# Sorting the partial products of a split-precision matmul: all high x high ones first

## The chip, the cores and the metric

The kernel runs on one core of a Trainium2 chip. The metric is the time of one execution on the device, in microseconds; the median of three runs stands for a kernel. Each kernel has one profiled execution besides, from which the trace and the profile page come. PE is TensorE (matmuls), DVE is VectorE, ACT is ScalarE, POOL is GpSimd, SP is the engine that issues most of the DMAs.

## The reference

A decoder trunk of two layers over 512 tokens of width 1024, in fp32. Layer 0 mixes tokens by attention with a forget gate, layer 1 by a gated short convolution. Each layer then has an MLP of width 4096 with squared ReLU and a gate stage that adds a per-layer embedding. Cut to what matters here:

```python
def sq_relu_mlp(h, w_up, w_down):
    return jnp.square(jax.nn.relu(h @ w_up)) @ w_down

for i in range(DEPTH):                                  # DEPTH = 2
    ...                                                 # mixer, residual
    f = sq_relu_mlp(rmsnorm(x, g[2]), w_mlp_up[i], w_mlp_down[i])
    x = x + rmsnorm(f, g[3])
    gate = jax.nn.sigmoid(rmsnorm(x, g[4]) @ w_ple_gate[i])
    e = (p[i] @ w_ple_proj[i]) * gate
    x = x + rmsnorm(e, g[5])
```

## The kernel before

**Split products.** Every fp32 operand is split into a high part, which ACT makes with a cast (line 272), and a low part, the difference, which DVE or POOL makes with a subtraction (line 273); a `Pair` holds both. A product is three matmuls into one PSUM bank, which `mm3` issues for one term after another: high x high (line 264), low x high (line 265), high x low (line 266). Names in the trace end in h and l for the two parts: wh and wl are a weight's, hTh and hTl those of the normed, transposed hidden state, A12h and A12l those of a quarter of the activations.

**The MLP** goes in 8 groups of 512 of the 4096 hidden columns. `up` makes four blocks f = 0 to 3 of 128 hidden columns each; block f takes 8 terms (k = 0 to 7) into a bank `up`. Group 0 does this in two chunks of 256 tokens, all four blocks of the first chunk and then all of the second; the other groups take all 512 tokens at once. ACT empties the bank with a ReLU into a page r (line 820) and squares r into a page q (line 806).

For groups 0 to 6 the down-projection is a scheme of seven products in place of eight (Strassen-Winograd). Its left factors are quarters of the activations and their sums: A11, A12, A22 and S1 to S4; blocks 0 and 1 give the first tile of each, blocks 2 and 3 the second (the last) tile. `quarters` has POOL make the sums s (line 834), and `halves` splits them. Its right factors are quarters of the weights and their sums T1 to T4, which POOL makes in `derive` (line 167) and of which POOL also makes the low parts. `down` runs the steps in the order `STEPS` = (1, 2, 4, 5, 6, 7, 3); each step is one product: two halves of tokens s, each with a bank `dn`, and two tiles p, four terms or 12 matmuls of 512 columns in all. Step 1 takes A11, steps 2 and 4 the quarters A12 and A22, which are split together under the name A12, step 5 takes S1, step 6 S2, split with S1, and steps 7 and 3 take S3 and S4. In group 0 ACT copies the finished banks into pages acc (line 863), in groups 1 to 6 DVE adds them to acc (line 866). Group 7 is plain and `combine` puts the products together.

**The gate stage** `ple` runs 8 blocks in the order `BLOCKS`, 8 terms each into a bank `pg`.

**What sets the order.** There are 8 PSUM banks, given out in turn, so a new step needs a bank that an earlier result has left. The MLP and gate stages aren't ordered by hand: a scheduler takes the program as written, with an estimate of its times, and moves each engine's instructions; each engine then works its list off in order, waiting on semaphores. Weights are fetched and split ahead of use: `wide` and `narrow` name the weight wanted and have a number of further ones prepared (`prepare`), and `due` starts work that was put off for some number of streamed columns.

Of the kernel before, what the change touches and what calls it, by code (L numbers as in the profile page):

```python
# [15 lines left out]
P = 128  # L16
# [36 lines left out]
SEVENS = "cb"  # L53
QUARTERS = ("A11", "A12", "S2", "S1", "S3", "S4", "A22")
ON_POOL = ('S3', 'S4')


class Pair:
# [5 lines left out]
    def at(self, view):  # L64
        return Pair(view(self.hi), view(self.lo))
# [3 lines left out]
def trunk(ctx: ExitStack, tc, x, pT, g, wv, wqk, bf, wo, wci, wcq, cw, wco, wup, wdn, wpp, wpg, out):  # L69
# [128 lines left out]
    def narrow(*key, k, c, soon=SOON):  # L198

        c += k % 2 * 256  # L200
        return wide(*key, k // 2, soon=soon).at(lambda u: u[:, c : c + P])
# [52 lines left out]
    def due():  # L254
        while later and later[0][0] <= streamed[0]:
            later.pop(0)[2]()
# [5 lines left out]
    def mm3(ps, a, b, start, stop):  # L262

        nc.tensor.matmul(ps, a.hi, b.hi, start=start, stop=False)  # L264
        nc.tensor.matmul(ps, a.lo, b.hi, start=False, stop=False)  # L265
        nc.tensor.matmul(ps, a.hi, b.lo, start=False, stop=stop)  # L266
        streamed[0] += 3 * ps.shape[-1]
        due()

    def split(hi, lo, src, eng=nc.vector):  # L270

# [94 lines left out]
    def soon(t, n):  # L366

        return FEW if n else SOON
# [433 lines left out]
    def mlp(l, hT, xs, then, late):  # L802
        acc = {}

        def square(out, r):
            nc.scalar.activation(out, r, AF.Square)

        def up(gr, done, soon=lambda f: SOON):
            for lo, hi in ((0, 256), (256, 512)) if gr == 0 else ((0, 512),):
                n = hi - lo  # L810
                for f in range(4):
                    need(*range(lo // P, hi // P), *(range(NB) if f == 3 else ()))
                    ps = bank(f"up{l}_{gr}_{f}_{lo}")
                    for k in range(KT):
                        mm3(
                            ps[:, :n], narrow("up", l, 2 * gr + f // 2, k=k, c=f % 2 * P, soon=soon(f)),
                            hT.at(lambda h: h[:, k, lo:hi]), k == 0, k == KT - 1,
                        )
                    r = page(f"r{l}_{gr}_{f}_{lo}")
                    nc.scalar.activation(r[:, :n], ps[:, :n], AF.Relu)  # L820
                    done(f, lo, hi, r)

        def halves(gr, f, names, src, A):

            w = S // 2 * len(names)
            part = Pair(*(page(f"{names[0]}{s}{l}_{gr}_{f}", F32R) for s in "hl"))
            split(part.hi[:, :w], part.lo[:, :w], src[:, :w])
            for name, c in zip(names, (slice(0, S // 2), slice(S // 2, S))):
                A[name, f // 2] = part.at(lambda h: h[:, c])

        def quarters(gr, f, q, s, A):

            L, R = slice(0, S // 2), slice(S // 2, S)
            sums = lambda out, a, b, op: nc.gpsimd.tensor_tensor(out=out, in0=a, in1=b, op=op)
            if f % 2 == 0:
                s[f] = page(f"s34{l}_{gr}_{f}")
                sums(s[f][:, L], q[f][:, L], q[f][:, R], ALU.subtract)
                return
            left, right = q[f - 1], q[f]
            halves(gr, f, ("A12", "A22"), right, A)  # L840
            s12, s34 = page(f"s12{l}_{gr}_{f}"), s[f - 1]
            sums(s12[:, L], left[:, R], right[:, R], ALU.add)
            sums(s12[:, R], s12[:, L], left[:, L], ALU.subtract)
            sums(s34[:, R], right[:, L], s12[:, R], ALU.subtract)
            halves(gr, f, ("S1", "S2"), s12, A)
            halves(gr, f, ("S3", "S4"), s34, A)

        def down(gr, A):

            for i in STEPS:  # L850
                a_name, b_name = PRODUCTS[i]
                banks = [bank(f"dn{l}_{gr}_{i}{s}") for s in range(2)]
                for p in range(2):
                    w = wide("dn", l, gr, b_name, p)
                    for s in range(2):
                        mm3(
                            banks[s], A[a_name, p].at(lambda h: h[:, s * P : (s + 1) * P]), w,
                            p == 0, p == 1,
                        )
                for s in range(2):  # L860
                    if gr == 0:
                        acc[i, s] = page(f"acc{l}_{i}_{s}")
                        nc.scalar.copy(acc[i, s][:, :S], banks[s])
                    else:
                        a = acc[i, s][:, :S]
                        nc.vector.tensor_tensor(out=a, in0=banks[s], in1=a, op=ALU.add)  # L866

        def combine():

            for s in range(2):  # L870
                for to, i in ((2, 1), (6, 1), (7, 6), (4, 7), (6, 5), (3, 6), (5, 7)):
                    a = acc[to, s][:, :S]
                    nc.gpsimd.tensor_tensor(out=a, in0=a, in1=acc[i, s][:, :S], op=ALU.add)  # L873
            return {
                (2 * half + s, n): acc[i, s]
                for s in range(2) for i, half, n in ((2, 0, 0), (3, 0, 1), (4, 1, 0), (5, 1, 1))
            }

        for gr in range(7):
            A, s, q = {}, {}, {f: page(f"q{l}_{gr}_{f}") for f in range(4)}  # L880

            def done(f, lo, hi, r):
                square(q[f][:, lo:hi], r[:, : hi - lo])
                if lo == 0 and f % 2 == 0:
                    halves(gr, f, ("A11",), q[f], A)
                if hi == S:
                    quarters(gr, f, q, s, A)

            up(gr, done)
            down(gr, A)  # L890

        total, hs, gB = combine(), [], []

        def done(f, lo, hi, r):
            h = Pair(*(page(f"h{s}{l}_{f}", F32R) for s in "hl"))
            nc.scalar.activation(h.hi[:, :S], r[:, :S], AF.Square)
            sq = page(f"q{l}_{f}")
            square(sq[:, :S], r[:, :S])
            nc.vector.tensor_tensor(
                out=h.lo[:, :S], in0=sq[:, :S], in1=h.hi[:, :S].bitcast(F32), op=ALU.subtract  # L900
            )
            hs.append(h)
            if f == LATE:
                gB.extend(late())

        up(7, done, lambda f: SOON + 2 * f)
        for t in range(NB):
            banks = [bank(f"dn{l}_7_{t}_{n}") for n in range(2)]
            for f, n in [(f, n) for f in range(4) for n in range(2)] if t == 0 else [
                (f, n) for n in range(2) for f in range(4)  # L910
            ]:
                w = wide("dn", l, 7, n, f, soon=14)
                mm3(banks[n], tokens_of(hs[f], t), w, f == 0, f == 3)
            for n in range(2):
                a = total[t, n][:, :S]
                nc.vector.tensor_tensor(out=a, in0=banks[n], in1=a, op=ALU.add)
            fs = [total[t, n][:, :S] for n in range(2)]
            sums = [squares(f, f"fs{l}_{t}_{n}") for n, f in enumerate(fs)]
            mg = [gained(f, gB, n, None, total[t, n]) for n, f in enumerate(fs)]
            residual(t, mg, sums, xs[t], f"mr{l}")  # L920
            then(t)

    def ple(l, hT, xs, gB, then):
# [15 lines left out]
        for t, n in BLOCKS:  # L939
            need(t)  # L940
            if (t, n) == (2, 0):
                prepare(where["pg", l, 1, KT - 1] + 1 + SOON)
            pe = early.pop(0) if early else None
            if pe is None and l == 1 and (t, n) == BLOCKS[-1]:
                pe = proj(t, n)
            ps = bank(f"pg{l}_{n}_{t}")
            for k in range(KT):
                w = wide("pg", l, n, k, soon=soon(t, n))
                mm3(ps, tokens(hT, k, t), w, k == 0, k == KT - 1)
            gate = page(f"gate{l}_{n}_{t}")  # L950
            nc.scalar.activation(gate[:, :S], ps, AF.Sigmoid)
            pe = pe or proj(t, n)
            e = page(f"e{l}_{n}_{t}")
            nc.vector.tensor_tensor(out=e[:, :S], in0=pe, in1=gate[:, :S], op=ALU.mult)
            sums[t, n] = squares(e[:, :S], f"es{l}_{n}_{t}")
            mgs[t, n] = gained(e[:, :S], gB, n, f"em{l}_{n}_{t}")
            if (t, 1 - n) in mgs:
                residual(t, *([d.pop((t, i)) for i in range(2)] for d in (mgs, sums)), xs[t],
                         f"er{l}")
                then(t)  # L960
# [141 lines left out]
```

## Time and the profile before

| | |
|---|---|
| median of 3 runs | 1234.35 us (1234.16 to 1234.91) |
| profiled execution | 1234.05 us, its span 1232.3 us |
| mean granted TensorE clock | 0.998 |
| PE, DVE, ACT, POOL busy | 1211.7, 898.9, 676.6, 680.3 us |
| matmuls on PE | 6188 |
| time PE waited, by the waits view, for operands in the down-projection | 2.6 us |

The rows shown below are lines of the profile page and of answers of the trace. A row of a timeline has the start and the busy time in us, the engine, the line of the kernel, the operation, output <- inputs, partitions x elements, and xN where N instructions stand together. A bracket gives the idle time before it and what ended it, as inferred from the semaphores. Ends of matmuls are modelled and overlap the next start; the distance between starts is what counts.

### The profile page before, as it was taken

The numbers are of one execution on the slowest core, as the hardware profiler recorded it, in microseconds if no ns is written. First come the engines' busy times: TensorE is split into PE (matmuls) and PEld (weight loads), VectorE is DVE, ScalarE is ACT, GpSimd is POOL, SyncE is SP. The second block draws the span as 40 slices with busy tenths as digits, with TensorE's granted clock in tenths as the row PEclk, the third lists the DMA queues.
The fourth block names the chain that finished last, engine by engine and source line by source line (L and its number), as shares of the span: only waits on it lengthen the run. The fifth ranks groups of instructions, "written<-read, shape, count | busy, mean of one in ns | idle before, by whom it ended". The sixth has DMA issues, their size and how long they took to land.

```text
span 1232.3 us, 18654 instructions
## 1 busy us (share of the span) xinstructions
PE 1211.7 (98%) x6188; PEld 1029.5 (84%) x6188; DVE 898.9 (73%) x1394; ACT 676.6 (55%) x1429; POOL 680.3 (55%) x635
## 2 busy tenths in 40 slices
PE   7999999999999999999999999999999999999997
PEld 6888888898788888888889999989878888888886
DVE  5658878675688767869877798865674787669873
ACT  5457778557634654455566534445756445635551
POOL 2016657147977787775213255317778868778210
PEclk9999999999999999999999999999999999999999
DMA  7456555532343224428123033552421443235401
GB/s 256 151 156 170 151 161 122 188 117 85 96 137 111 85 78 137 134 68 301 53 95 112 27 103 97 161 170 69 137 81 57 137 137 96 67 113 179 163 18 52
DMA packets 85793, 148.73 MB, mean 121 GB/s; under 512 B 10112, under 2 KB 17328, under 8 KB 85696
## 3 DMA queue, kind: packets, MB, share of 16 engines
q1 hardware_dynamic: 85488, 147.27, 39.0%
q8 instruction: 49, 0.80, 0.3%
q14 instruction: 48, 0.39, 0.1%
q10 hardware_dynamic: 144, 0.26, 0.1%
q0 software_dynamic: 64, 0.00, 0.0%
HBM read 136.93 MB, written 6.37 MB: 116 GB/s over the span
## 4 chain that ended last, share of the span: by engine, by line
PE 91%; DVE 3%; ACT 2%; POOL 2%; DMA 1%; issue 1%; SPq 0%; DVEq 0%; POOLq 0%; ACTq 0%
PE up L266 9%; PE up L265 9%; PE up L264 9%; PE dn L265 8%; PE dn L266 8%; PE dn L264 8%; PE qk L265 2%; PE qk L264 2%; PE qk L266 2%; PE pg L265 2%; PE pg L266 2%; PE pg L264 2%; PE pT L539 1%; PE n_p L312 1%; PE co L264 1%; PE co L265 1%
## 5 line engine op out<-in xcount | busy, mean ns | idle before, releaser
L273 DVE TENSOR_TENSOR wl<-raw,wh 128x512 fp32r<-128x512 f32 (+1 forms) x398 | 372.4, 980 | 27.3 <-ACT wh L272 26.2
L272 ACT CAST wh<-raw 128x512 fp32r<-128x512 f32 (+1 forms) x398 | 217.5, 619 | 4.6 <-DVE xd L348 4.4
L266 PE MATMUL up<-hTl,wh 128*128 128x512 f32 (+1 forms) x576 | 209.7, 366 | 0.6 <-DVE hTl L273 0.6
L265 PE MATMUL up<-hTh,wl 128*128 128x512 f32 (+1 forms) x576 | 210.2, 365 | 0.0
L264 PE MATMUL up<-hTh,wh 128*128 128x512 f32 (+1 forms) x576 | 209.4, 366 | 0.0
L273 POOL TENSOR_TENSOR wl<-dn_T,wh 128x512 fp32r<-128x512 f32 x112 | 154.7, 1414 | 32.6 <-ACT wh L272 32.6
L820 ACT ACTIVATE r<-up 128x512 f32<-128x512 f32 (+1 forms) x72 | 39.5, 548 | 199.2 <-PE up L266 199.2
L866 DVE TENSOR_TENSOR acc<-dn,acc 128x512 f32<-128x512 f32 x168 | 107.2, 679 | 23.5 <-PE dn L266 23.5
L266 PEld LDWEIGHTS up<-hTl,wh 128*128 128x128 f32 x576 | 108.3, 189 | 18.2 <-DVE hTl L273 0.8
L264 PEld LDWEIGHTS up<-hTh,wh 128*128 128x128 f32 x576 | 108.7, 189 | 17.6
L265 PEld LDWEIGHTS up<-hTh,wl 128*128 128x128 f32 x576 | 108.6, 189 | 17.5
L167 POOL TENSOR_TENSOR dn_T<-raw,raw 128x512 f32<-128x512 f32 x56 | 87.9, 1582 | 59.8 <-DMA raw<-in_wdn 49.7
L167 POOL TENSOR_TENSOR dn_T<-raw,dn_T 128x512 f32<-128x512 f32 x56 | 92.7, 1656 | 2.2
L272 ACT CAST wh<-dn_T 128x512 fp32r<-128x512 f32 x112 | 61.4, 616 | 11.1 <-POOL dn_T L167 11.1
L273 DVE TENSOR_TENSOR A12l<-q,A12h 128x512 fp32r<-128x512 f32 x28 | 23.6, 844 | 50.2 <-ACT A12h L272 50.2
L273 DVE TENSOR_TENSOR A11l<-q,A11h 128x256 fp32r<-128x256 f32 x28 | 25.6, 914 | 45.9 <-ACT A11h L272 45.9
L873 POOL TENSOR_TENSOR acc<-acc,acc 128x512 f32<-128x512 f32 x28 | 46.9, 1709 | 9.9 <-DVE acc L866 9.9
L265 PE MATMUL qk<-hTh,wl 128*128 128x512 f32 x128 | 51.0, 399 | 0.0
L266 PE MATMUL qk<-hTl,wh 128*128 128x512 f32 x128 | 51.0, 398 | 0.0
L264 PE MATMUL qk<-hTh,wh 128*128 128x512 f32 x128 | 50.9, 398 | 0.0
L265 PE MATMUL pg<-wh,hTl 128*128 128x512 f32 x128 | 50.5, 394 | 0.0
L264 PE MATMUL pg<-wh,hTh 128*128 128x512 f32 x128 | 50.4, 394 | 0.0
(370 smaller groups left out, 3231.5 us busy)
## 6 DMA issues: line engine op xcount, KB each, us to landing
raw<-in_wup SPq DMA_DIRECT2D x128, 256.0 KB, 3.1
raw<-in_wdn SPq DMA_DIRECT2D x128, 256.0 KB, 2.9
raw<-in_wcq SPq DMA_DIRECT2D x36, 256.0 KB, 2.8
raw<-in_wqk SPq DMA_DIRECT2D x32, 256.0 KB, 3.8
raw<-in_wpg SPq DMA_DIRECT2D x32, 256.0 KB, 4.6
g<-in_g SPq DMA_DIRECT2D x22, 256.0 KB, 6.2
prl<-neg_c SPq DMA_DIRECT2D x16, 256.0 KB, 7.0
raw<-in_wo SPq DMA_DIRECT2D x16, 256.0 KB, 5.8
```

Source lines behind the costliest of these rows:

```text
L167: ins = nc.gpsimd.tensor_tensor(out=B[name], in0=B[a], in1=B[b], op=op)
L264: nc.tensor.matmul(ps, a.hi, b.hi, start=start, stop=False)
L265: nc.tensor.matmul(ps, a.lo, b.hi, start=False, stop=False)
L266: nc.tensor.matmul(ps, a.hi, b.lo, start=False, stop=stop)
L272: nc.scalar.copy(hi, src)
L273: eng.tensor_tensor(out=lo, in0=src, in1=hi.bitcast(F32), op=ALU.subtract)
L312: nc.tensor.transpose(ps[:, j * P : (j + 1) * P], h[:, j * P : (j + 1) * P], ident)
L539: nc.tensor.transpose(ps[:, b * P : (b + 1) * P], probs[h][b][:, j * P : (j + 1) * P], ident)
L820: nc.scalar.activation(r[:, :n], ps[:, :n], AF.Relu)
L866: nc.vector.tensor_tensor(out=a, in0=banks[s], in1=a, op=ALU.add)
L873: nc.gpsimd.tensor_tensor(out=a, in0=a, in1=acc[i, s][:, :S], op=ALU.add)
```

## The change

A helper `products` takes a list of terms and an order of parts, and issues all matmuls of one kind over all terms before those of the next kind. It takes the place of `mm3` in three places: in every step of `down` (order: high x high, high activations x low weights, low activations x high weights), in the two chunks of group 0 in `up` (high x high, low weights x high hidden state, high weights x low hidden state), and in the first block of the gate stage. A step of `down` so issues 4 + 4 + 4 matmuls over both tiles, where it was 3 for each term. The weights of a step are asked for together ahead of its first matmul, and `due` is called after each matmul instead of after three. The number of matmuls, their shapes and the banks are the same.

```diff
+LOW_A_LAST = (("hi", "hi"), ("hi", "lo"), ("lo", "hi"))
+LOW_B_LAST = (("hi", "hi"), ("lo", "hi"), ("hi", "lo"))
...
+    def products(terms, order, closed=True):
+
+        parts = [(getattr(a, p), getattr(b, q), ps) for p, q in order for ps, a, b in terms]
+        first, last = {}, {}
+        for i, (_, _, ps) in enumerate(parts):
+            first.setdefault(id(ps), i)
+            last[id(ps)] = i
+        for i, (a, b, ps) in enumerate(parts):
+            nc.tensor.matmul(
+                ps, a, b, start=i == first[id(ps)], stop=closed and i == last[id(ps)]
+            )
+            streamed[0] += ps.shape[-1]
+            due()
...
-                    for k in range(KT):
-                        mm3(
-                            ps[:, :n], narrow("up", l, 2 * gr + f // 2, k=k, c=f % 2 * P, soon=soon(f)),
-                            hT.at(lambda h: h[:, k, lo:hi]), k == 0, k == KT - 1,
-                        )
+                    at = lambda k: (
+                        narrow("up", l, 2 * gr + f // 2, k=k, c=f % 2 * P, soon=soon(f)),
+                        hT.at(lambda h: h[:, k, lo:hi]),
+                    )
+                    if gr == 0:
+                        out = ps[:, :n]
+                        products([(out, *at(k)) for k in range(KT)], LOW_B_LAST)
+                    else:
+                        for k in range(KT):
+                            mm3(ps[:, :n], *at(k), k == 0, k == KT - 1)
...
-                for p in range(2):
-                    w = wide("dn", l, gr, b_name, p)
-                    for s in range(2):
-                        mm3(
-                            banks[s], A[a_name, p].at(lambda h: h[:, s * P : (s + 1) * P]), w,
-                            p == 0, p == 1,
-                        )
+                ws = [wide("dn", l, gr, b_name, p) for p in range(2)]
+                products([
+                    (banks[s], A[a_name, p].at(lambda h: h[:, s * P : (s + 1) * P]), ws[p])
+                    for p in range(2) for s in range(2)
+                ], LOW_A_LAST)
...
-            for k in range(KT):
-                w = wide("pg", l, n, k, soon=soon(t, n))
-                mm3(ps, tokens(hT, k, t), w, k == 0, k == KT - 1)
+            if (t, n) == BLOCKS[0]:
+                w = [wide("pg", l, n, k, soon=soon(t, n)) for k in range(KT)]
+                products([(ps, tokens(hT, k, t), w[k]) for k in range(KT)], LOW_A_LAST)
+            else:
+                for k in range(KT):
+                    w = wide("pg", l, n, k, soon=soon(t, n))
+                    mm3(ps, tokens(hT, k, t), w, k == 0, k == KT - 1)
```

## The prediction

> **What bounds the kernel now.** I read the page first: the busy shares, then the chain that ended last.
>
> ```profile
> span 1232.3 us, 18654 instructions
> ...
> PE 1211.7 (98%) x6188; PEld 1029.5 (84%) x6188; DVE 898.9 (73%) x1394; ACT 676.6 (55%) x1429; POOL 680.3 (55%) x635
> ...
> PE 91%; DVE 3%; ACT 2%; POOL 2%; DMA 1%; issue 1%; SPq 0%; DVEq 0%; POOLq 0%; ACTq 0%
> ```
>
> TensorE is busy for 98% of the span and holds 91% of the chain. The change neither adds nor removes a matmul: the two built programs hold the same instructions on every engine, each as often, and differ in order alone. So a new order can only take away places where PE stands still, or make new ones. Where it stands still now is in the waits of PE (engine and line, what was waited for: us in total, times, longest):
>
> ```profile
> PE dn L264 <- ACT r L820: 1.2, 2, 0.9
> ...
> PE dn L265 <- DVE S1l L273: 0.8, 2, 0.4
> ...
> PE dn L265 <- DVE A12l L273: 0.4, 1, 0.4
> ...
> PE dn L264 <- ACT A12h L272: 0.2, 1, 0.2
> ```
>
> All waits of the down-projection (dn) are in this list: 2.6 us together. The same view cut to 345 to 660 us, which is groups 2 to 6 of the first MLP and what follows it, is empty. So the places where the order can matter are few: group 0 and group 1 of each layer, and the first up-projection chunk. To turn matmuls into time I take the cadence from the chain, four matmuls of 512 columns in 0.91 us, 0.2275 us each (start to start; the durations that the timeline gives overlap):
>
> ```profile
> 278.75 1.74 POOL dn_T L167
> ...
> 287.08 1.89 POOL s L834 x2
> ...
> 293.41 1.20 PE dn L264 x4
> ...
> 347.66 0.91 PE dn L266 x4
> ```
>
> The first three rows say more: in group 0 of layer 0 the chain leaves PE. It runs over POOL, which makes the summed weights T and their low parts, and after them the sums s of the activations' quarters; only at 293.41 does it come back to PE. This stretch is set by POOL and ACT, however PE is ordered.
>
> **Group 0, the large term.** PE in this stage as it is now (start, busy us, then the bracket with the wait):
>
> ```profile
> 285.03 0.63 PE L264 MATMUL dn<-wh,A11h 128*128 128x512 f32 x2
> ...
> 290.27 0.39 PE L266 MATMUL dn<-wl,A12h 128*128 128x512 f32 x1
> 291.58 0.50 PE L264 MATMUL dn<-wh,S1h 128*128 128x512 f32 x1 [0.92 <-ACT r L820]
> ...
> 293.41 1.20 PE L264 MATMUL dn<-wh,A12h 128*128 128x512 f32 x4 [0.15 <-ACT A12h L272]
> ...
> 297.39 0.39 PE L266 MATMUL dn<-wl,S1h 128*128 128x512 f32 x1
> ...
> 298.06 0.40 PE L265 MATMUL dn<-wh,S1l 128*128 128x512 f32 x1
> ```
>
> From 285.03 to 290.27 it runs 24 matmuls: 12 of step 1 and 12 on A12 of the first tile (4 high x high, 8 with a low part, for steps 2 and 4). Then it waits for a PSUM bank: step 5 takes the bank that the relu r of the second chunk has to empty. It does 6 on S1 and comes at 293.41 to A12 of the last tile. So 30 are done before 293.41. What ACT does meanwhile, and why the relu is late:
>
> ```profile
> 290.63 0.62 ACT L272 CAST S3h<-s 128x512 fp32r<-128x512 f32 x1 [0.21 <-POOL s L834]
> 291.15 0.38 ACT L820 ACTIVATE r<-up 128x256 f32<-128x256 f32 x1
> ...
> 292.74 0.62 ACT L272 CAST A12h<-q 128x512 fp32r<-128x512 f32 x1
> ```
>
> ACT takes its work in order: the relu stands behind the cast of S3h, which waits for POOL's sum, and A12h of the last tile stands behind both relus. POOL's and ACT's order in this stage is the same in both programs, and the T sums wait for no matmul of the changed steps, so 291.15 and 292.74 stay.
>
> The changed order of this stage is: the 12 of step 1, sorted; 4 high x high on A12 of the first tile; 2 high x high on S1 of the first tile, which need the banks that ACT's last two relus empty, the first at 291.5; then A12h of the last tile. The 8 matmuls of A12 with low parts, which now keep PE busy up to 290.5, are sorted behind the last tile's high x high ones, since a step's parts go over both tiles; so are the 4 of S1. By 293.41 PE has done 12 + 4 + 2 = 18 instead of 30. The hole between 285.03 + 16 x 0.2275 = 288.67 and 291.58 is 2.9 us wide. Twelve matmuls have to be made up: 12 x 0.2275 = 2.73 us. A small wait goes away: from 297.39 to 298.06 are two intervals, 0.67 against 0.455, so 0.215 is lost now and is not later, because all operands are then long ready. Net +2.5 us in layer 0. Nothing later takes it back: group 1 follows on a PE that does not wait at its start.
>
> Layer 1 has the same stage:
>
> ```profile
> 858.86 1.07 PE L264 MATMUL dn<-wh,A12h 128*128 128x512 f32 x4
> ...
> 861.98 0.50 PE L264 MATMUL dn<-wh,S1h 128*128 128x512 f32 x1 [0.24 <-ACT r L820]
> ...
> 863.80 1.19 PE L264 MATMUL dn<-wh,A12h 128*128 128x512 f32 x4
> ```
>
> The hole is 858.86 + 0.91 = 859.77 to 861.98, 2.2 us, and the count at 863.80 is 18 instead of 30 again: +2.5 us.
>
> **The first up-projection chunk.** In layer 0 the first matmul that reads the low part of the hidden state, the seventh of the chunk, waits for VectorE:
>
> ```profile
> 260.87 0.39 PE L266 MATMUL up<-hTl,wh 128*128 128x256 f32 x1 [0.64 <-DVE hTl L273]
> ```
>
> Sorted, the products with hTl come last, behind 16 others, and the wait goes. It gains nothing at the end of group 0: what PE saves here it stands still for in the hole, since 291.58 is set by POOL and ACT. The cover of this edit is that hole; without it, it would be worth the 0.64 us of the bracket or a little more. Layer 1 has no such wait.
>
> **Group 1, the gain.** Both layers wait for low parts that VectorE makes late:
>
> ```profile
> 334.58 1.07 PE L264 MATMUL dn<-wh,A12h 128*128 128x512 f32 x4
> ...
> 338.75 0.50 PE L265 MATMUL dn<-wh,S1l 128*128 128x512 f32 x1 [0.39 <-DVE S1l L273]
> 339.09 0.40 PE L266 MATMUL dn<-wl,S1h 128*128 128x512 f32 x1
> ...
> 904.99 1.07 PE L264 MATMUL dn<-wh,A12h 128*128 128x512 f32 x4
> ...
> 909.39 0.50 PE L265 MATMUL dn<-wh,S1l 128*128 128x512 f32 x1 [0.38 <-DVE S1l L273]
> ```
>
> Between the first row and S1l lie 14 matmuls, 3.19 us of cadence; 4.17 pass in layer 0 and 4.40 in layer 1. After a wait the next one comes 0.34 instead of 0.23 later (338.75 to 339.09). So 0.98 + 0.11 = 1.1 us are lost in layer 0 and 1.21 + 0.11 = 1.3 in layer 1. Why VectorE is late:
>
> ```profile
> 333.65 1.29 DVE L866 TENSOR_TENSOR acc<-dn,acc 128x512 f32<-128x512 f32 x2 [5.19 <-PE dn L266]
> 334.86 0.88 DVE L273 TENSOR_TENSOR A12l<-q,A12h 128x512 fp32r<-128x512 f32 x1
> ```
>
> The low part stands behind two additions to acc, which wait 5.19 us for PE. In the changed program A12l and S1l of the last tile stand ahead of these additions, and PE reads them later, in the last third of a step. Both reasons work the same way: the whole wait goes, -1.1 and -1.3.
>
> **Groups 2 to 6, gate.** No wait there to remove; could there be a new one? A step now wants A12h of the last tile about 18 matmuls after the down stage begins:
>
> ```profile
> 451.31 0.39 PE L264 MATMUL dn<-wh,A11h 128*128 128x512 f32 x1
> ...
> 452.81 0.62 ACT L272 CAST A12h<-q 128x512 fp32r<-128x512 f32 x1
> ```
>
> Here (group 4) it is ready at 453.43 and wanted at 451.31 + 18 x 0.2275 = 455.4: 2 us to spare. I take 0; the bound on the other side is one settling interval, 0.11 us, in 10 groups, +1.1. The first gate block has no wait now: 0.
>
> **The sum.** +2.5 + 2.5 - 1.1 - 1.3 = +2.6 us on the profiled execution, which took 1234.05 us (span 1232.3). The median of the runs is 1234.35, 0.3 above it. So 1234.35 + 2.6 = 1236.9 us.
>
> **The rivals.** (a) *The clock.* Holes of 2.9 and 2.2 us are new on PE in mid-run. What an empty PE does to the granted clock shows at the end, in windows (us, busy time of PE, PEld, DVE, ACT, POOL, granted clock, DMA share, GB/s):
>
> ```profile
> 1224.00:1227.70 3.70, 0.41 (x2) 0.00 (x0) 1.42 (x3) 1.32 (x3) 0.86 (x2) 1.00 0.00 0
> 1227.70:1232.30 4.60, 0.00 (x0) 0.00 (x0) 1.38 (x2) 0.00 (x0) 0.00 (x0) 0.51 0.30 114
> ```
>
> PE is empty for 3.3 us (3.70 - 0.41) with the clock at 1.00, then 0.51. So 2.9 us is just short of what is shown to be harmless, and 2.2 us well short. If the clock fell in layer 0 and stayed down for another 3.3 us at half speed, that is my estimate +1.7 us: 1238.6; in both layers 1240.3. [...] (b) *The waits of group 1 stay*, because VectorE is held by something else: without -2.4 the time is 1239.3. Against it: the bracket names only these additions. (c) *The other side: POOL's chain runs faster, and the hole shrinks.* The T sums take uneven times:
>
> ```profile
> 269.88 2.55 POOL L167 TENSOR_TENSOR dn_T<-raw,raw 128x512 f32<-128x512 f32 x2 [1.58 <-DVE n_h L303]
> ...
> 275.34 3.44 POOL L167 TENSOR_TENSOR dn_T<-raw,raw 128x512 f32<-128x512 f32 x2
> ```
>
> The same pair takes 2.55 or 3.44 us. If all eight ran like the first two, this chain would end up to 1.7 us earlier in each layer, 291.58 and 293.41 with it, and the cost of group 0 would fall to 0.8: 1234.35 + 1.6 - 2.4 = 1233.5, not slower. It decides from 1.3 us earlier a layer, where the sum is zero. Against it: nothing that shares the time with POOL there has changed place. (d) *The change doesn't do what it says*: excluded, the order of the built program is what I counted.
>
> **How the numbers follow.** The forecast has 0.62, with its own range 1236.2 to 1237.7 (0.35 a layer for group 0, some tenths for group 1). The clock (a) has 0.12, the waits that stay (b) 0.10, the other side (c) 0.16. A measurement of this kernel can tell about 0.2%, 2.5 us, from no change: slower is above 1236.8, faster below 1231.9. The forecast lies on that line: 0.33 of it above, 0.29 below. Slower: 0.33 + 0.12 + 0.10 = 0.55. Of (c), 0.05 is for the hole closing wholly and the 0.64 of the first chunk showing, 1234.35 - 2.4 - 0.64 = 1231.3, faster; the rest, 0.11, and the lower part of the forecast make the same: 0.40. The range reaches from the middle of (c), 1234.4, over one layer of (a), 1238.6, and (b), 1239.3, with half of the bound of groups 2 to 6 on top, 1239.8.
>
> **What would show it.** In the changed profile PE should stand still from about 288.2 to 291.6 and from 859.8 to 862.0 (shifted by what happened before), with a bracket that names ACT's r on the first matmul of S1h, and A12h of the last tile should start near 293.4. The waits for A12l and S1l in group 1 should be gone, the additions to acc stand behind the low parts on VectorE, and the stage that starts at 334.58 begins 2.5 us later. The granted clock should stay at 1.00 behind both holes. The prediction is wrong if the hole is under 2 us, if groups 2 to 6 show waits of PE for A12h or S1l, or if matmuls behind the hole take 0.45 us each.

## The result: 1243.11 us, slower by more than three times what was forecast

| | before | changed |
|---|---|---|
| median us (6 runs each, side by side) | 1234.26 (1233.08 to 1235.06) | 1243.11 (1241.53 to 1243.36) |
| ratio to before | 1 | 1.0071 (95%: 1.0060 to 1.0082) |
| profiled execution, span us | 1234.05, 1232.3 | 1242.21, 1240.5 |
| mean granted TensorE clock | 0.998 | 0.995 |

The kernel got slower, as forecast, but by 8.85 us where 2.6 were forecast, and the time lies outside the range given (1234.4 to 1239.8). The waits of PE in the changed profile, the lines that answer to those shown of before and the new ones (line numbers are the changed kernel's: L280 is the matmul in `products`, L841 the relu, L288 and L289 the casts and subtractions of `split`):

```profile
PE dn L280 <- ACT r L841: 5.1, 4, 2.7
PE dn L280 <- ACT A12h L288: 1.4, 3, 0.6
PE c L266 <- DVE za L772: 1.1, 1, 1.1
...
PE c L267 <- DVE wl L289: 0.6, 1, 0.6
...
PE c L266 <- ACT wh L288: 0.5, 1, 0.5
```

The waits for S1l, A12l and hTl in the MLP are gone, as forecast. The wait for ACT's relu grew from 1.2 to 5.1 us. Three waits at the convolution (c) stand in this list; of these before had only that for za, 0.7 us.

To see where the time went I compare when PE starts the same matmul in two profiles. The table has the start in a profile less the start in before's, in us; the difference of two neighbouring columns is what a stage cost.

| profile | group 0 down, layer 0 | group 1 up | gate stage | convolution, a later c | MLP, layer 1 | group 1 up, layer 1 | gate stage, layer 1 | last gate block |
|---|---|---|---|---|---|---|---|---|
| start in before | 285.03 | 306.02 | 595.47 | 684.18 | 831.34 | 876.43 | 1166.10 | 1218.81 |
| changed | -0.61 | 3.66 | 2.53 | 5.47 | 5.48 | 9.49 | 8.14 | 8.17 |
| gate alone | 0.01 | 0.00 | 0.28 | 3.02 | 3.04 | 3.02 | 3.02 | 3.04 |
| down alone | 0.02 | 4.98 | 3.86 | 3.91 | 3.91 | 6.35 | 5.00 | 5.00 |
| ten fillers | -0.62 | 2.32 | 1.19 | 3.93 | 3.94 | 6.40 | 5.05 | 5.08 |
| sorted within tiles | 0.09 | 0.64 | -0.49 | 2.23 | 2.24 | 2.34 | 0.99 | 1.02 |

The row of the changed kernel: group 0 with the chunk ahead of it costs 3.66 us in layer 0 and 4.0 in layer 1 (forecast 2.5 each), group 1 gives back 1.1 and 1.35 (forecast 1.1 and 1.3), and 2.9 us are lost from the gate stage to the convolution (forecast 0). The other rows are the experiments below.

Group 0 of layer 0 on PE in the changed kernel (timeline):

```profile
287.49 1.19 PE L280 MATMUL dn<-wh,A12h 128*128 128x512 f32 x4 [0.16 <-ACT A12h L288]
291.37 0.50 PE L280 MATMUL dn<-wh,S1h 128*128 128x512 f32 x1 [2.69 <-ACT r L841]
292.09 0.50 PE L280 MATMUL dn<-wh,S1h 128*128 128x512 f32 x1 [0.22 <-ACT r L841]
293.19 1.22 PE L280 MATMUL dn<-wh,A12h 128*128 128x512 f32 x2 [0.60 <-ACT A12h L288]
294.21 1.91 PE L280 MATMUL dn<-wl,A12h 128*128 128x512 f32 x4
295.92 0.75 PE L280 MATMUL dn<-wh,A12l 128*128 128x512 f32 x2
```

The hole is there: four products on A12h, then nothing until 291.37, and A12h of the last tile at 293.19 (forecast 291.58 and 293.4). What was not forecast is the next row: four matmuls from 294.21 to 295.92, 0.43 us each instead of 0.2275. The windows of the changed profile show why (columns as in the prediction; the seventh figure, after the busy times, is the granted clock):

```profile
288.00:291.30 3.30, 0.69 (x3) 0.20 (x2) 1.11 (x3) 1.50 (x3) 2.23 (x3) 1.00 0.00 0
291.30:293.90 2.60, 1.72 (x4) 0.99 (x5) 1.15 (x2) 1.74 (x5) 1.98 (x3) 0.78 0.00 0
293.90:296.30 2.40, 2.40 (x8) 1.88 (x7) 1.04 (x2) 1.62 (x3) 1.29 (x2) 0.53 0.00 0
296.30:299.00 2.70, 2.70 (x13) 2.23 (x12) 0.34 (x1) 2.70 (x7) 2.48 (x2) 1.00 0.03 6
...
869.80:873.20 3.40, 3.40 (x9) 2.59 (x9) 1.49 (x3) 2.49 (x5) 2.07 (x3) 0.53 0.00 0
```

PE is full from 293.90 to 296.30, but the granted clock is 0.53, and 8 matmuls fit where before's profile has 13 in the same stretch:

```profile
293.90:296.30 2.40, 2.40 (x13) 1.95 (x12) 0.99 (x3) 1.40 (x3) 1.52 (x2) 1.00 0.00 0
```

Layer 1 has the same. Where the clock falls and rises is not where these windows are cut: it is 0.50 from 292.76 to 296.17 and from 869.62 to 873.03, 3.41 us each time (rows under "Behind which idle time the clock fell"). By the excess over the cadence the two slow stretches cost 1.4 and 1.6 us.

The new wait at the convolution: the last input of layer 1 (`n0b_h`, on VectorE) is 5.5 us later than before, while PE is 2.6 us later when it enters the convolution (first c: 655.42 before, 657.98 after). Before's row first, then the changed kernel's:

```profile
662.33 1.41 DVE L303 SCALAR_TENSOR_TENSOR n0b_h<-xd,n0b_r_y,g 128x512 f32<-128x512 f32 x2 [1.99 <-POOL n0b_r_y L290]
```

```profile
667.79 1.42 DVE L319 SCALAR_TENSOR_TENSOR n0b_h<-xd,n0b_r_y,g 128x512 f32<-128x512 f32 x2 [1.98 <-POOL n0b_r_y L306]
```

### The profile page after: what moved, and what is told of

The parts are those of the page before. It is cut to its first block, busy times and chain, and to the rows that moved or that the text cites. A ratio compares the mean times of both kernels' runs of the same rounds, so it can differ in the third digit from the quotient of the medians.

```text
span 1240.5 us, 18681 instructions
## 1 busy us (share of the span) xinstructions
PE 1215.2 (98%) x6188; PEld 1032.5 (83%) x6188; DVE 910.1 (73%) x1394; ACT 676.7 (55%) x1429; POOL 676.3 (55%) x635
## 4 chain that ended last, share of the span: by engine, by line
PE 90%; ACT 2%; DVE 2%; POOL 2%; issue 2%; DMA 1%; SPq 0%; DVEq 0%; POOLq 0%; ACTq 0%
PE dn L280 21%; PE up L268 8%; PE up L267 8%; PE up L266 8%; PE up L280 3%; PE qk L267 2%; PE qk L266 2%; PE qk L268 2%; PE pT L555 1%; PE n_p L328 1%; PE pg L267 1%; PE pg L266 1%; PE pg L268 1%; PE o L266 1%; PE o L268 1%
## 5 line engine op out<-in xcount | busy, mean ns | idle before, releaser
L289 DVE TENSOR_TENSOR wl<-raw,wh 128x512 fp32r<-128x512 f32 (+1 forms) x398 | 386.1, 1017 | 27.6 <-ACT wh L288 26.8
L288 ACT CAST wh<-raw 128x512 fp32r<-128x512 f32 (+1 forms) x398 | 217.1, 617 | 4.6 <-DVE xd L364 4.4
L267 PE MATMUL up<-hTh,wl 128*128 128x512 f32 x448 | 174.3, 389 | 0.0
L268 PE MATMUL up<-hTl,wh 128*128 128x512 f32 x448 | 174.3, 389 | 0.0
L266 PE MATMUL up<-hTh,wh 128*128 128x512 f32 x448 | 174.3, 389 | 0.0
L289 POOL TENSOR_TENSOR wl<-dn_T,wh 128x512 fp32r<-128x512 f32 x112 | 151.3, 1383 | 32.6 <-ACT wh L288 30.1
L841 ACT ACTIVATE r<-up 128x512 f32<-128x512 f32 (+1 forms) x72 | 39.4, 547 | 215.8 <-PE up L268 215.8
L267 PEld LDWEIGHTS up<-hTh,wl 128*128 128x128 f32 x448 | 84.1, 188 | 17.5
L266 PEld LDWEIGHTS up<-hTh,wh 128*128 128x128 f32 x448 | 84.1, 188 | 17.5
L268 PEld LDWEIGHTS up<-hTl,wh 128*128 128x128 f32 x448 | 84.1, 188 | 17.4
L289 DVE TENSOR_TENSOR A12l<-q,A12h 128x512 fp32r<-128x512 f32 x28 | 19.4, 694 | 68.8 <-ACT A12h L288 68.8
L288 ACT CAST wh<-dn_T 128x512 fp32r<-128x512 f32 x112 | 61.4, 616 | 11.5 <-POOL dn_T L169 11.5
L289 DVE TENSOR_TENSOR A11l<-q,A11h 128x256 fp32r<-128x256 f32 x28 | 23.1, 823 | 45.3 <-ACT A11h L288 45.3
L303 POOL TENSOR_SCALAR n_r_v<-n_q,n_q 128x1 f32<-128x1 f32 x20 | 6.0, 300 | 74.9 <-ACT junk L311 74.9
L855 POOL TENSOR_TENSOR s<-q,q 128x256 f32<-128x256 f32 x28 | 21.6, 771 | 43.0 <-ACT q L822 43.0
```

What stands on the lines that cost most here:

```text
L288: nc.scalar.copy(hi, src)
L289: eng.tensor_tensor(out=lo, in0=src, in1=hi.bitcast(F32), op=ALU.subtract)
```

## The experiments

**Which edit costs what.** Four kernels, one part of the change each. For the first:

```diff
 (down-projection and up-projection as before)
+            if (t, n) == BLOCKS[0]:
+                w = [wide("pg", l, n, k, soon=soon(t, n)) for k in range(KT)]
+                products([(ps, tokens(hT, k, t), w[k]) for k in range(KT)], LOW_A_LAST)
```

> Only the first gate block of each layer is sorted; the down-projection and the up-projection are as before. Theory (the sorted gate block itself costs the start of layer 1): ACT's casts of the hidden state come ahead of the first sigmoid, the chain of small operations that makes layer 1's input gets later, and PE waits at the start of the convolution for it: about +2.7 us, 1237.0. Rival (the wait at the convolution comes from the delays in the MLP, the gate edit is free): 1234.3, no new wait there.

Measured: 1236.9 us, ratio 1.0023 (1.0014 to 1.0032) to before's 1234.3. The edit costs 2.6 us by itself, and all of it at the convolution (row "gate alone" of the table: 0.28 at the gate stage, 3.02 behind it). The sort itself moves the schedule: a version of the program that asks for the eight weights ahead but keeps the old order of matmuls has every engine's list as before (that version was built, not run). In the gate stage ACT now takes the casts of the last hidden state and of a weight ahead of the first sigmoid. ACT in before, then in this kernel:

```profile
619.83 0.60 ACT L951 ACTIVATE gate<-pg 128x512 f32<-128x512 f32 x1
620.33 0.58 ACT L272 CAST hTh<-n_p 128x512 fp32r<-128x512 f32 x1
```

```profile
619.19 0.59 ACT L288 CAST hTh<-n_p 128x512 fp32r<-128x512 f32 x1 [0.37 <-PE n_p L328]
619.68 0.62 ACT L288 CAST wh<-raw 128x512 fp32r<-128x512 f32 x1
620.32 1.28 ACT L971 ACT_TABLE_LOAD   x1
621.61 0.60 ACT L971 ACTIVATE gate<-pg 128x512 f32<-128x512 f32 x1
```

The first sigmoid is 1.8 us later, though PE begins the block's last matmul at 608.0 in before and at 608.3 here. From there on DVE, ACT and POOL work a serial chain, token block by token block (product, squares, normalization, next product), with a second swap of this kind further on (ACT takes casts and copies ahead of the sigmoid that before starts at 648.24; it comes at 651.14), and its end comes late:

```profile
665.34 1.41 DVE L319 SCALAR_TENSOR_TENSOR n0b_h<-xd,n0b_r_y,g 128x512 f32<-128x512 f32 x2 [1.99 <-POOL n0b_r_y L306]
```

3.0 us after before's 662.33. That the edit costs this is shown; that the swap on ACT carries it is read from the trace and was not tried by itself. The second:

```diff
 (up-projection and gate as before)
+                products([
+                    (banks[s], A[a_name, p].at(lambda h: h[:, s * P : (s + 1) * P]), ws[p])
+                    for p in range(2) for s in range(2)
+                ], LOW_A_LAST)
```

> Only the steps of the down-projection are sorted, in all seven groups; the first up-projection chunks and the gate as before. Theory: the hole in group 0 (+2.5 a layer) and the lower clock behind it (+1.5 a layer), less 2.4 in group 1: about +5.7 us, 1240.0, and no new wait at the start of the convolution. Rival (the convolution's wait comes from the MLP's delay): about +8.5, 1242.8.

Measured: 1239.5 us, ratio 1.0043 (1.003 to 1.0056): +5.2, no new wait at the convolution (3.86 to 3.91 in the table). But the clock fell in another way than in the changed kernel (windows as above):

```profile
291.30:293.90 2.60, 1.79 (x3) 0.96 (x4) 1.19 (x2) 1.97 (x5) 1.75 (x3) 0.63 0.00 0
293.90:296.30 2.40, 2.40 (x7) 1.82 (x7) 1.01 (x3) 1.39 (x3) 1.51 (x2) 0.50 0.00 0
296.30:299.00 2.70, 2.70 (x9) 2.08 (x8) 0.57 (x1) 2.70 (x6) 2.26 (x2) 0.54 0.00 0
...
868.40:870.80 2.40, 2.40 (x13) 1.95 (x12) 1.03 (x2) 1.62 (x3) 1.29 (x2) 1.00 0.00 0
```

In layer 0 it stays down for 6.83 us instead of 3.41; in layer 1 it does not fall, behind a hole as wide as the changed kernel's (2.2 us). Layer 1's group 0 costs 2.44 here (6.35 - 3.91): that is the 2.5 of the prediction, at full clock. Layer 0's costs 4.96, so 2.5 for the clock. That the sum comes near the expected 1240.0 is luck: 1.5 was expected in each layer, and it was 2.5 in one and nothing in the other. The third:

```diff
 (down-projection and gate as before)
+                    if gr == 0:
+                        out = ps[:, :n]
+                        products([(out, *at(k)) for k in range(KT)], LOW_B_LAST)
```

> Only the two up-projection chunks of group 0 are sorted. Theory: the wait for the low hidden part at 260.87 goes, but the time returns as a longer wait in the down-projection of group 0, which is set by POOL and ACT: 0, 1234.3. Rival (it is a gain of its own): -0.9, 1233.4.

Measured: 1234.87 us, ratio 1.0004 (0.9996 to 1.0013): no change. The wait for hTl is gone from its list, and the time comes back in group 0, whose down-projection takes 0.4 us more by the starts (0.15 us earlier than before's at 285.03, 0.25 later at 306.02). It does not come back as a longer wait for the relu, which is 1.2 us as before. The fourth:

```diff
+                if gr > 0:
+                    products([ ... ], LOW_A_LAST)
+                else:
+                    (steps as before)
```

> The down-projection is sorted in groups 1 to 6 alone; group 0, the up-projection and the gate as before. Theory: the waits of group 1 go (-1.1 and -1.3) and nothing else changes: -2.4, 1231.9. Rival (sorting costs something in every group, for example by the change of bank after each matmul): no gain, 1234.3 or more.

Measured: 1232.14 us, ratio 0.9981 (0.9972 to 0.9990): faster by 2.2. The waits for S1l and A12l are gone, and no other wait of the down-projection is changed. Sorting costs nothing in a group whose operands are early.

**The clock.** Ten matmuls in the hole that nothing reads:

```diff
+                if gr == 0 and i == 2:
+                    for _ in range(10):
+                        nc.tensor.matmul(
+                            banks[0], A[a_name, 0].hi[:, :P], ws[0].hi, start=True, stop=True
+                        )
```

> The changed kernel with ten matmuls more in group 0 of each layer, ahead of step 2: they repeat its first product into its own bank, which the step then starts anew, so they are 20 matmuls or 4.6 us of work that nothing reads. Theory (PE empty in the hole lowers the clock behind it): the extra work fits into the hole, A12h of the last tile still starts when ACT has it, and the slow stretches behind the holes (1.4 and 1.6 us lost) go: 1243.1 - 3.0 = 1240.1, faster with more work. Rival (the slow matmuls behind the hole come from their operands or from the sorted order): the slow stretches stay, 1243.1 or later.

Measured: 1239.34 us, ratio 1.0042 (1.0029 to 1.0056) to before's 1234.47; 3.8 us faster than the changed kernel with 20 matmuls more. PE in its profile:

```profile
287.48 2.58 PE L877 MATMUL dn<-wh,A12h 128*128 128x512 f32 x10 [0.16 <-ACT A12h L288]
289.90 1.07 PE L280 MATMUL dn<-wh,A12h 128*128 128x512 f32 x4
291.41 0.50 PE L280 MATMUL dn<-wh,S1h 128*128 128x512 f32 x1 [0.44 <-ACT r L841]
...
293.23 0.73 PE L280 MATMUL dn<-wh,A12h 128*128 128x512 f32 x2 [0.60 <-ACT A12h L288]
293.80 1.09 PE L280 MATMUL dn<-wl,A12h 128*128 128x512 f32 x4
```

S1h still starts at 291.41 and A12h at 293.23, to 0.05 us where they were: the hole is set by ACT, and the filler cost nothing. The four matmuls from 293.80 take 0.23 us each, and the clock is 1.00 in group 0 of both layers (windows from 288.0 to 299.0 and from 866.0 to 873.2). So the slow stretch came from PE standing empty. Half the filler:

```diff
-                    for _ in range(10):
+                    for _ in range(5):
```

> The changed kernel with five matmuls more in group 0 of each layer, placed and unread as the ten of the experiment before: holes of some 1.7 and 1.0 us are left. Theory (PE must be mostly empty over some 3 us before the clock falls): the part left is short enough, 1239 to 1240, as with ten. Rival (any hole above 1.5 us is enough, as layer 1's 1.4 us was when VectorE made the low parts): the slow stretch stays in layer 0, about 1241.5.

Measured: 1241.18 us, ratio 1.0060 (1.0046 to 1.0074). The rival's number. In its profile the clock falls in layer 0, behind a hole of 1.7 us, and not in layer 1, behind one of 1.1:

```profile
293.90:296.30 2.40, 2.40 (x7) 1.91 (x6) 1.19 (x2) 1.77 (x4) 1.14 (x2) 0.50 0.00 0
...
868.40:870.80 2.40, 1.79 (x8) 1.25 (x8) 0.69 (x1) 1.01 (x3) 2.24 (x4) 1.00 0.00 0
```

**The hole.** Sorting within a tile in group 0:

```diff
+                if gr == 0:
+                    (all three parts of terms[:2], the first tile)
+                    (all three parts of terms[2:], the last tile)
+                else:
+                    products(terms, LOW_A_LAST)
```

> The changed kernel, but in group 0 of each layer a step sorts its parts within a tile: all three parts of the first tile, then those of the last. Theory (the hole comes from sorting over both tiles): hole and slow stretch go, group 0 costs as before, 1243.1 - 2 x (2.5 + 1.5) = 1235.1. Rival (sorting as such, by changing the bank after each matmul, disturbs group 0): 1240 or more.

Measured: 1235.19 us, ratio 1.0006 (0.9997 to 1.0014), to 0.1 us what was expected. Group 0 costs 0.55 us in layer 0 and 0.1 in layer 1, the clock stays at 1.00: 8 us came from sorting over both tiles alone. What is left of the change is the gain of group 1 and the loss at the gate. What sets the hole was asked with POOL unburdened:

```diff
-            eng = nc.gpsimd if key[0] == "dn" or key[-1] in ON_POOL else nc.vector
+            eng = nc.gpsimd if key[0] == "dn" and key[2] > 0 or key[-1] in ON_POOL else nc.vector
```

> The changed kernel with the low parts of group 0's summed weights T made by VectorE instead of POOL. Theory (the hole is set by POOL's row of T sums, low parts and quarter sums ahead of ACT's relu): POOL reaches the quarter sums up to 5.2 us earlier, the hole closes and the clock holds: up to 8 us less, 1235 to 1237. Rival (ACT or the end of the up-projection sets the hole): less than 2 us of change, 1241 or more.

Measured: 1239.89 us, ratio 1.0047 (1.0034 to 1.0059); 3.2 us less than the changed kernel, where up to 8 were expected. Its runs spread from 1238.44 to 1243.48, and the profiled one is the slowest; there the clock is down for 6.83 us in layer 0, for 3.41 in layer 1 and, far ahead of the MLP, for 3.41 from 16.97 on. POOL and ACT in it:

```profile
288.04 0.75 POOL L855 TENSOR_TENSOR s<-q 128x256 f32<-128x256 f32 x1 [4.39 <-ACT q L822]
```

```profile
290.69 0.62 ACT L288 CAST S1h<-s 128x512 fp32r<-128x512 f32 x1 [1.36 <-POOL s L855]
```

POOL now stands idle for 4.39 us until ACT has squared the last block: the quarter sums cannot begin earlier, since they need the end of the up-projection. The relu still stands behind them on ACT, and PE still has a hole of 2.0 us and 1.4 us. The theory held for about a third of the hole (0.8 us in each layer); the rest is the chain from the end of the up-projection over ACT, POOL and ACT again. The two shorter holes make 1.6 of the 3.2 us; the other half is open, since the only trace is of the slowest run.

**Behind which idle time the clock fell.** The same idle time, a wait of 2.0 us for the relu and then 0.22 and 0.60 us around two lone matmuls, was followed by a fall of the clock in layer 1 of the changed kernel and by none in layer 1 with the down-projection alone. The traces of these runs show one difference. In each fall of group 0 the low clock lasted 3.41 us or twice that, 6.83. In the changed kernel's profile the two low stretches have 3.413 us each, the full clock between them lasts 573.44 us, and the full clock from there to the fall at the end of the run, at 1234.84, lasts 361.81 us: 168 and 106 times 3.413, to within 0.1 us. So its falls lie on one grid of 3.413 us from layer 0 to the end. The falls of layer 0 begin at 292.76 in this profile, at 291.95 with the down-projection alone, at 293.45 with VectorE making the low parts and at 293.80 with five fillers. Windows cut along the grid of a profile show what PE did ahead of a fall. The changed kernel in both layers:

```profile
289.35:292.76 3.41, 1.01 (x2) 0.37 (x2) 1.38 (x2) 2.86 (x7) 1.87 (x4) 1.00 0.00 0
292.76:296.17 3.41, 2.98 (x7) 2.41 (x8) 1.60 (x3) 1.86 (x4) 2.35 (x3) 0.50 0.00 0
...
866.20:869.62 3.42, 1.40 (x4) 0.72 (x5) 1.80 (x3) 2.70 (x7) 1.88 (x4) 1.00 0.00 0
869.62:873.03 3.41, 3.41 (x10) 2.63 (x9) 1.67 (x3) 2.32 (x5) 2.08 (x3) 0.50 0.00 0
```

The down-projection alone in layer 1, on the grid of its own fall at 291.95:

```profile
861.98:865.39 3.41, 1.86 (x9) 1.20 (x7) 1.33 (x2) 1.10 (x2) 2.74 (x4) 1.00 0.00 0
865.39:868.80 3.41, 2.12 (x7) 1.31 (x8) 1.44 (x3) 2.14 (x6) 2.39 (x3) 1.00 0.00 0
868.80:872.21 3.41, 3.41 (x17) 2.81 (x16) 1.39 (x2) 3.03 (x6) 2.08 (x3) 1.00 0.00 0
```

In the changed kernel the idle time lies in one window, which keeps 1.40 us of work; here a boundary of the grid cuts it in two, and each window keeps more. The windows of group 0 with the least work, in order:

| profile and layer | PE busy, us of 3.41 | clock in the next window |
|---|---|---|
| down alone, 0 | 0.70 | 0.50 |
| changed, 0 | 1.01 | 0.50 |
| VectorE making the low parts, 0 | 1.33 | 0.50 |
| changed, 1 | 1.40 | 0.50 |
| five fillers, 0 | 1.76 | 0.50 |
| VectorE making the low parts, 1 | 1.77 | 0.50 |
| down alone, 1 | 1.86, then 2.12 | 1.00 |
| five fillers, 1 | 2.34 | 1.00 |
| ten fillers, 0 and 1 | 2.58 and 2.60 | 1.00 |

All other windows at full clock between 20 and 1200 us had 2.30 us or more in the changed kernel's profile and 2.49 or more in before's, and there was no fall behind any of them. So a fall came behind windows with 0.70 to 1.77 us of work, and none behind those at full clock with 1.86 or more. That the same hole can do either, by where the grid cuts it, is the author's reading of these rows: the busy times rest on modelled ends, and no run moved a hole against the grid and changed nothing else. It fits that runs of one kernel differ: the four with five fillers took from 1240.63 us at a mean clock of 0.997 to 1243.45 at 0.995.

**The gate by layer.**

```diff
-            if (t, n) == BLOCKS[0]:
+            if l == 1 and (t, n) == BLOCKS[0]:
```

> Only the first gate block of layer 1 is sorted, everything else as before. Theory (the gate's cost is the late input of the next layer's convolution, which layer 1 does not have behind it): 1234.3, no change. Rival (the sorted gate block costs in its own stage, through ACT's order): half of what the two layers' edit cost, +1.3, 1235.6.

Measured: 1234.25 us, ratio 1.0000 (0.9991 to 1.0009). Layer 1's gate block costs nothing; the 2.6 us are layer 0's alone, where a mixer waits behind it.

**A version that beats both.** The down-projection sorted in groups 1 to 6, the rest as before, and VectorE making group 0's low parts of T:

> The down-projection sorted in groups 1 to 6 alone, group 0, the up-projection and the gate in the order of before, and VectorE making the low parts of T in group 0. Theory: the 2.2 us of groups 1 stay won, and the small waits of group 0 (1.8 in layer 0, 1.1 in layer 1) go too: 1229.2. Rival (VectorE becomes late with other low parts in group 0): 1232 or more.

Measured: 1229.87 us, ratio 0.9962 (0.9950 to 0.9975), 4.6 us less than before's 1234.47 and 13 less than the changed kernel. No wait of the down-projection is left in its list of waits; in PE's steps the wait for S1h in layer 0 is 0.24 us (1.08 before). By the starts, group 0 becomes 0.8 us shorter in layer 0 and 0.9 in layer 1, where 1.8 and 1.1 were expected: POOL's head start is worth what it took off the hole of the sorted group, 0.8 a layer. The old order of parts still fills the time until ACT is ready. With the up-projection sorted too:

> The fastest version so far (down-projection sorted in groups 1 to 6 alone, gate as before, VectorE making the low parts of T in group 0) with the up-projection chunks of group 0 sorted as well. Theory (what the chunk saves is taken back by the wait for ACT and POOL in the down-projection behind it): no change, 1229.9. Rival (with POOL out of the way the 0.3 to 0.9 us show): 1229.2.

Measured: 1230.35 us, ratio 0.9968 (0.9955 to 0.9980): no gain over the version without.

## Why the prediction was wrong: its steps one by one

- **Group 0, the hole: right.** PE has nothing from 288.5 to 291.37 in layer 0, 2.9 us as forecast, 18 matmuls are done at 293.19 as counted, and where the clock held the stage cost 2.44 us (down alone, layer 1; the ten fillers give 2.46 there). The T sums did not change.
- **The clock: the step that failed.** The prediction read the end of before's trace, 3.3 us of empty PE at full clock, as a bound below which a hole is harmless, looked at each hole by itself, and gave a fall of the clock 0.12 of the chances; its range leaves out a fall in both layers. It fell in both. The row at the end does not show that 3.3 us are harmless. Cut where the clock falls, at 1227.80, before's end is a stretch of 3.41 us with 0.02 us of work, at full clock, and the low clock behind it:

```profile
1224.39:1227.80 3.41, 0.02 (x1) 0.00 (x0) 1.52 (x3) 1.32 (x3) 0.86 (x2) 1.00 0.00 0
1227.80:1231.21 3.41, 0.00 (x0) 0.00 (x0) 1.28 (x2) 0.00 (x0) 0.00 (x0) 0.50 0.40 154
```

The 3.3 us are the time until the clock fell here, no bound for a hole in mid-run. Nor did lone matmuls keep the clock up: after the hole of layer 0 PE ran two single matmuls with 0.5 and 0.9 us lost between them, so it was idle for 4.2 us of the 4.7 from 288.5 to 293.2, and had 1.01 us of work in the 3.41 us ahead of the fall. The low clock then lasted 3.41 us in each layer. The price for a layer, +1.7, was right in size (1.4 and 1.6) for a fall of 3.41 us.
- **The gate: the other step that failed.** "The first gate block has no wait now: 0" looked at PE alone. The stage is not bound by PE at its end: a serial chain on DVE, ACT and POOL makes layer 1's input, and PE reaches the convolution just as that is ready. The swaps on ACT were to be seen in the order of the built program, ahead of the first sigmoid; the edit costs 2.6 to 2.9 us, by the trace through these swaps.
- **The first chunk: right**, worth nothing, alone and in the fastest version.
- **Group 1: right**, -1.1 and -1.35 in the trace, -2.2 in the run of its own. Of its two reasons one held in part: in layer 0 A12l (333.60) stands ahead of the two additions (335.27) on VectorE, but S1l (336.48) still behind them. S1l is in time because PE reads it in the last third of its step, at 341.42.
- **Groups 2 to 6: right**, no wait there.
- **The other side** (POOL's chain faster) did not happen: the eight T sums take uneven times again, 12.1 us in all where before's take 12.0, and the experiment that freed POOL shows that it would have been worth less than assumed.

The sum with the two terms put right: 2.6 + 1.4 + 1.6 + 2.9 = 8.5, against 8.85 measured.

## What to carry to other kernels

Sorting partial products so that late operands come last helps where an operand is just late (here 2.2 us, groups 1 to 6); where a whole stage waits for a chain on other engines it takes away the very matmuls that filled the wait. Before pricing an empty stretch of PE, add up what PE still does over a stretch as long as the low clock lasted in these traces (3.41 us), lone matmuls and all, with the stretch in its worst position. Where 0.70 to 1.77 us were left here, the clock behind was 0.50, so price such a stretch twice: the hole, and the half clock behind it. An edit to PE's order alone still moves the lists of the other engines, and each swap ahead of a serial chain has to be followed to the chain's end, however far.

## What the runs showed of the hardware that was not expected

The granted clock fell to 0.50 for 3.41 or 6.83 us behind six windows of 3.41 us in group 0 in which PE had been busy for 0.70 to 1.77 us, and stayed at 1.00 behind those at full clock with 1.86 or more (table under "Behind which idle time the clock fell"). In the changed kernel's profile the stretches between its falls, 573.44 and 361.81 us, are whole multiples of the 3.413 us of its low stretches, to within 0.1. A hole of 1.4 us with 0.5 and 0.9 us lost behind it was followed by a fall in one kernel (VectorE making the low parts, layer 1), and one of 2.2 us with the same behind it was not in another (the down-projection alone, layer 1). Five matmuls in a hole of 2.9 us did not prevent the fall, ten did in the profiled run; one of the five runs with ten took 1241.14 us at a mean clock of 0.997, and no trace shows where. Why a fall lasted 3.41 us in one profile and 6.83 in another was not tried: the first 3.41 us of the two long falls had 2.90 and 2.88 us of work, the short ones 2.98 or more, too near each other to tell.
